# Seven products of half blocks in place of eight, in half of the second feed-forward product

## The chip, the cores and the metric

The kernel runs on one core of one Trainium2 chip. The metric is the device time of one execution in microseconds. Matrix products run on TensorE (PE in the rows; its weight loads are PEld), sums and differences mostly on VectorE (DVE), activations and copies on ScalarE (ACT); GpSimd (POOL) does little here. The weights are loaded by DMAs that SyncE's queue (SP) issues.

## The reference

Two layers, each a mixer and a feed-forward part, and a last RMSNorm, on x of 256 tokens by 1024 in float32. The mixer (dilated attention and an mLSTM, gated and merged) is untouched. The part that the change is about:

```python
SEQ, D_MODEL, D_FF, DEPTH = 256, 1024, 4096, 2
h2 = rms_norm(x, norm_mlp_w)
x = x + jnp.square(jax.nn.relu(h2 @ w_ff1)) @ w_ff2
```

`w_ff1` is 1024 x 4096, `w_ff2` is 4096 x 1024, of their own in each layer.

## The kernel before

**Products in three parts.** Each float32 operand of a large product is split into hi (a copy rounded to fp32r) and lo (the rest), and a product of two tiles is three matmuls: lo of the activations with hi of the weights, hi with hi, and hi with lo of the weights.

**Steps.** All large products go through one list of steps, each one weight tile of 128 x 2 x 512 elements (512 KB). `loads` (L403) issues its DMA into one of 6 buffers `raw`, `highs` (L429) makes `hi` on ScalarE, `lows` (L436) makes `lo` on VectorE, each in one of 5 buffers (`N_SPLIT`, `N_RAW`, L24), and TensorE runs the step's matmuls. So `hi` of step i waits until TensorE has finished step i - 5, and a load waits until `lo` has been made of the tile six before. All three walk the list in its order.

**The feed-forward part.** The hidden layer is cut into 8 blocks f of 512. The first product (`by_feature`, L446) keeps the weights stationary and streams the 256 tokens: 4 steps of 24 matmuls with 256 columns for a block, into two PSUM banks. `ff_evac` (L996) takes Relu and Square on ScalarE and splits the result into hi and lo tiles of the slot X. The second product (`by_token`, L487, with `token_products`, L478) keeps the hidden tiles stationary and streams 512 columns of `w_ff2`: per block 2 column halves c by 2 steps, each step 12 matmuls of 512 columns (2 token halves t, 2 tiles of the hidden dimension, 3 parts). It accumulates over all 8 blocks into four banks. The loop at L1147 interleaves: the second product of f, then the first of f + 2. `ff2_evac` adds the four sums to x, scaled by `r2`, the norm's factor per token.

**The order.** A planner in the kernel's own Python code sets each engine's order when the kernel is built. `Scheduler` (L257) holds tasks written as generators, `Plan` (L83) and `Timed` (L158) put a time on each instruction, and the earliest ready one is issued, with ranks among those that are near. An `Any` lets the planner choose the engine of a copy. On the chip each engine runs its list in that order, and semaphores make it wait for data and buffers.

## Time and profile before

| | us |
|---|---|
| median of 3 runs | 759.64 (759.34 to 759.66) |
| the profiled execution | 759.58 |
| its span, first to last instruction | 757.8 |
| TensorE busy | 749.6 |
| VectorE busy | 491.8 |
| ScalarE busy | 417.8 |

The page gives the busy time of each engine in the span, and in 40 slices of it. A matmul's row lasts longer than the distance to the next, because matmuls overlap in the array, so what one costs is read from starts. A row of waits says which engine's instruction ended an idle time. All instructions bear one line, L199 (a helper records them), so groups are told apart by their tiles.

### The profile page before, as it was taken

The page shows a single profiled execution, that of the slowest core. Times are in us where ns is not written, and L with a number is a line of the kernel's source. Part 1 is how long each engine was busy: PE and PEld are TensorE (multiplying, and loading weights), DVE is VectorE, ACT ScalarE, POOL GpSimd, SP SyncE. Part 2 cuts the span into 40 slices and gives each one's busy share as a digit, 9 for nine tenths or more (in the row PEclk, how much of TensorE's full clock was granted, in tenths as well). Part 3 has the DMA queues.
Part 4 walks back from the last instruction along what each step waited for, and adds up shares of the span by engine and source line. Part 5 has one row for each costly group of instructions (what it writes and reads, how often), then busy time and mean ns, then how long its engine had stood idle before and what let it go on. Part 6 is the DMA issues. An engine that isn't in the chain of part 4 may idle for free.

```text
span 757.8 us, 13082 instructions
## 1 busy us (share of the span) xinstructions
PE 749.6 (99%) x5195; PEld 689.0 (91%) x5195; DVE 491.8 (65%) x750; ACT 417.8 (55%) x662; POOL 53.3 (7%) x106
## 2 busy tenths in 40 slices
PE   9999999999999999999999999999999999999996
PEld 8989889998999988899899898899989899998895
DVE  5897986568664455555568988856766655445554
ACT  6657776445554445554456467745454654445552
POOL 4764010000000000000000000000000000000000
PEclk9999999999999999999999999999999999999999
DMA  9866554555456555555654654355565555555511
GB/s 309 287 193 210 171 155 140 186 179 190 169 175 203 181 190 195 181 185 191 194 164 127 216 179 139 117 177 181 186 209 184 180 188 189 191 182 189 194 57 55
DMA packets 71260, 136.16 MB, mean 180 GB/s; under 512 B 4792, under 2 KB 6752, under 8 KB 71200
## 3 DMA queue, kind: packets, MB, share of 16 engines
q1 hardware_dynamic: 69984, 133.63, 54.3%
q0 software_dynamic: 912, 1.41, 0.8%
q8 instruction: 40, 0.66, 0.3%
q10 hardware_dynamic: 304, 0.30, 0.1%
q14 instruction: 20, 0.16, 0.1%
HBM read 133.74 MB, written 1.05 MB: 178 GB/s over the span
## 4 chain that ended last, share of the span: by engine, by line
PE 97%; ACT 1%; DVE 1%; DMA 0%; SPq 0%; issue 0%; POOLq 0%; POOL 0%; DVEq 0%
PE bank L199 97%; DMA x<-in_x 0%; DVE x L199 0%; ACT hi L199 0%; ACT big L199 0%; ACT sg L199 0%; SPq L199 0%; DVE lo L199 0%; ACT slot0h L199 0%; DVE sg L199 0%; POOL small L199 0%; POOLq L1324 0%; DVE big L199 0%; DVE small L199 0%; DVEq L1324 0%
## 5 line engine op out<-in xcount | busy, mean ns | idle before, releaser
L199 DVE TENSOR_TENSOR lo<-raw,hi 128x1024 fp32r<-128x1024 f32 (+3 forms) x251 | 304.2, 1213 | 215.0 <-ACT hi L199 214.1
L199 ACT ACTIVATE hi<-raw 128x1024 fp32r<-128x1024 f32 (+3 forms) x251 | 262.7, 1048 | 269.9 <-PE bank L199 245.1
L199 PE MATMUL bank<-slot1l,hi 128*128 128x256 f32 x576 | 162.7, 282 | 0.0
L199 PE MATMUL bank<-slot1h,hi 128*128 128x256 f32 x576 | 162.4, 282 | 0.0
L199 PE MATMUL bank<-slot1h,lo 128*128 128x256 f32 x576 | 162.3, 282 | 0.0
L199 PE MATMUL bank<-slot0h,hi 128*128 128x256 f32 x576 | 161.7, 283 | 0.2 <-ACT hi L199 0.2
L199 PE MATMUL bank<-slot0h,lo 128*128 128x256 f32 x576 | 161.0, 283 | 0.2 <-DVE lo L199 0.2
L199 PE MATMUL bank<-slot0l,hi 128*128 128x256 f32 x576 | 161.0, 282 | 0.0
L199 PEld LDWEIGHTS bank<-slot1h,hi 128*128 128x128 f32 x576 | 108.4, 188 | 1.0 <-issue 0.5
L199 PEld LDWEIGHTS bank<-slot0h,hi 128*128 128x128 f32 x576 | 107.9, 188 | 1.4 <-ACT hi L199 0.4
L199 PEld LDWEIGHTS bank<-slot1l,hi 128*128 128x128 f32 x576 | 108.3, 188 | 0.8 <-issue 0.3
L199 PEld LDWEIGHTS bank<-slot1h,lo 128*128 128x128 f32 x576 | 108.5, 188 | 0.2 <-issue 0.2
L199 PEld LDWEIGHTS bank<-slot0h,lo 128*128 128x128 f32 x576 | 107.6, 188 | 0.9 <-issue 0.5
L199 PEld LDWEIGHTS bank<-slot0l,hi 128*128 128x128 f32 x576 | 107.9, 188 | 0.5 <-issue 0.2
L199 PE MATMUL bank<-hi,slot1h 128*128 128x512 f32 (+2 forms) x228 | 85.9, 377 | 0.0
L199 PE MATMUL bank<-hi,slot1l 128*128 128x512 f32 (+2 forms) x228 | 85.5, 375 | 0.0
L199 PE MATMUL bank<-lo,slot1h 128*128 128x512 f32 (+2 forms) x228 | 85.5, 375 | 0.0
L199 PE MATMUL bank<-hi,slot0h 128*128 128x512 f32 (+1 forms) x224 | 85.2, 380 | 0.0
L199 PE MATMUL bank<-lo,slot0h 128*128 128x512 f32 (+1 forms) x224 | 84.9, 379 | 0.0
L199 PE MATMUL bank<-hi,slot0l 128*128 128x512 f32 (+1 forms) x224 | 84.8, 379 | 0.0
L199 PEld LDWEIGHTS bank<-lo,slot1h 128*128 128x128 f32 x228 | 42.8, 188 | 8.2
L199 PEld LDWEIGHTS bank<-hi,slot1h 128*128 128x128 f32 x228 | 42.8, 188 | 8.1 <-issue 0.3
(156 smaller groups left out, 718.7 us busy)
## 6 DMA issues: line engine op xcount, KB each, us to landing
raw<-in_w_ff SPq DMA_DIRECT2D x128, 512.0 KB
raw<-in_w_in SPq DMA_DIRECT2D x78, 512.0 KB
raw<-in_w_out SPq DMA_DIRECT2D x16, 512.0 KB
raw<-in_w_in SPq DMA_DIRECT2D x8, 520.0 KB
raw<-in_w_proj_mlstm SPq DMA_DIRECT2D x8, 512.0 KB
raw<-in_w_proj_att SPq DMA_DIRECT2D x8, 512.0 KB
raw<-in_w_in SPq DMA_DIRECT2D x3, 256.0 KB
x<-in_x SPq DMA_DIRECT2D x3, 256.0 KB
```

Of the source, the lines that this page charges most:

```text
L199: f(*args, **kw)
```

## The change

The 512 hidden units of a block, the 256 tokens and the 1024 output columns are each halved. Then the second product of a block is a 2 x 2 matrix of half blocks (128 tokens by 256 hidden units) times a 2 x 2 matrix of half blocks (256 by 512): eight half-block products of 6 matmuls each. For the blocks f = 0, 2, 4, 6 (`BY_SEVEN`) the kernel now uses Winograd's form of Strassen's scheme: seven products of sums of half blocks. Odd blocks stay as they were.

- The four half blocks of the hidden layer are written by Square into `mqk` (free in this part of the layer); `sums` makes four differences and sums of them on VectorE, 256 columns each, and splits all seven stationary operands into `q_h` (in the place of `zc`) and `q_l` (in the place of `sg0`), in a piece of four and one of three. There is one `q_h` and one `q_l`: the next even block waits until the last product has been made.
- The weights of a block are four tiles b11, b12, b21, b22. Three of the seven products take them as loaded (b11, b22, b21), one takes b12 + b22 (t3, formed in b12's `raw` buffer), three take running sums in `mog` (t1 = b11 + b12, t2 = t1 + b22, t4 = t2 + b21). `weight_sums` forms these four on VectorE, 1024 columns each. Each of the seven is a step of its own with a hi and a lo, and 6 matmuls.
- The products accumulate over the even blocks into seven banks, so that one bank is left. After the last even block `flush` combines P1, P6, P7 and p5 and adds them to x: three copies on ScalarE, four sums and four updates of x on VectorE. The banks of p2, p3 and p4 go on as accumulators of the odd blocks, with one more.
- The first product of blocks 2 to 7 is done in half blocks of 256 hidden units (`by_feature_half`): 2 steps of 24 matmuls, one bank, weight tiles loaded as 128 x 4 x 256 (runs of 1 KB where there were 2 KB).
- The order of steps, for f = 0, 2, 4: half block of f + 2, b11, t1, half, t3, b22, half, t2, b21, half, t4. For f = 6 the place of the halves is taken by the second product of blocks 1 and 3; blocks 5 and 7 follow. In each layer only the planner's numbers for step lengths (`new_step`) and tiles that share a place (`Tenants`) are new besides. In the last layer the final norm's weights are loaded after `flush`.

The core of the diff:

```diff
+    def by_feature_half(w, c0, xs, st, evac):
+        xh, xl = xs
+        for q in range(2):
+            def fn(i, hi, lo, q=q):
+                if q == 0:
+                    st["b"], = yield Take(banks)
+                yield Need(("hi", i))
+                order = [(kt, blk, n) for blk in range(2) for kt in range(4) for n in range(3)]
+                for j, (kt, blk, n) in enumerate(order):
+                    at["part"] = j / len(order)
+                    if n == 2:
+                        yield Need(("lo", i))
+                    k = 4 * q + kt
+                    yield mm(st["b"][:, blk * S:(blk + 1) * S], (hi, hi, lo)[n][:, kt, blk * P:(blk + 1) * P],
+                             (xh, xl, xh)[n][:, k, :], q == 0 and blk == 0 and kt == 0 and n == 0,
+                             q == 1 and kt == 3 and n == 2)
+                if q == 1:
+                    add(evac(st["b"]), 1)
+            src = w.rearrange("(k p) c -> p k c", p=P)[:, 4 * q:4 * q + 4, c0:c0 + 256]
+            new_step(src, lambda t: flat_of(t)[:, 0:1024].rearrange("p (k c) -> p k c", k=4), 2.84, fn)
...
-        hid = lambda f: tuple(s[:, 4 * (f % 2):4 * (f % 2) + 4, :] for s in X)
+        def hidden():
+            yield Need(*[tag(f"mix{k}") for k in range(4)])
+            shared.hidden()
+            mark(tag("hidden"))
+        def hid(f):
+            if f in shared.hid:
+                return shared.hid[f]
+            return tuple(s[:, 4 * (f // 2 - 2):4 * (f // 2 - 2) + 4, :] for s in X)
...
+        q_all = mqk.rearrange("p (n j) (t u) -> p (n j t) u", j=1, u=P).rearrange("p (n j) u -> p n j u", j=2)
...
-                yield act.activation(a[:], a[:], AF.Square)
-                hh, hl = (s[:, 2 * b:2 * b + 2, :] for s in hid(f))
-                yield Any(vec.tensor_copy(hh, halves(a)), act.activation(hh, halves(a), AF.Copy))
-                yield vec.tensor_tensor(hl, halves(a), hh, op=OP.subtract)
+                if f in BY_SEVEN:
+                    if f > BY_SEVEN[0]:
+                        yield Need(tag(f"q{f - 2}"))
+                    part = a.rearrange("p (j t u) -> p t j u", j=2, t=2)
+                    yield act.activation(q_all[:, 0:8:7] if b == 0 else q_all[:, 1:3], part, AF.Square)
+                else:
+                    yield act.activation(a[:], a[:], AF.Square)
+                    yield Need(tag("hidden"))
+                    hh, hl = (s[:, 2 * b:2 * b + 2, :] for s in hid(f))
+                    yield Any(vec.tensor_copy(hh, halves(a)), act.activation(hh, halves(a), AF.Copy))
+                    yield vec.tensor_tensor(hl, halves(a), hh, op=OP.subtract)
...
+        def sums(f):
+            yield Need(tag("hidden"), tag(f"f{f}0"), tag(f"f{f}1"), *([tag(f"seven{f - 2}")] if f > BY_SEVEN[0] else []))
+            q = [q_all[:, n] for n in range(8)]
+            yield vec.tensor_tensor(q[3], q[7], q[2], op=OP.subtract)
+            yield vec.tensor_tensor(q[6], q[0], q[7], op=OP.subtract)
+            yield vec.tensor_tensor(q[4], q[3], q[0], op=OP.subtract)
+            yield vec.tensor_tensor(q[5], q[4], q[1], op=OP.add)
+            for a, b in ((0, 4), (4, 7)):
+                yield Any(act.activation(shared.q_h[:, a:b], q_all[:, a:b], AF.Copy), vec.tensor_copy(shared.q_h[:, a:b], q_all[:, a:b]))
+                yield vec.tensor_tensor(shared.q_l[:, a:b], q_all[:, a:b], shared.q_h[:, a:b], op=OP.subtract)
+            mark(tag(f"q{f}"))
+        def weight_sums(f, i, raw):
+            b11, b12, b21, b22 = (wide(512)(raw[n].raw) for n in ("b11", "t3", "b21", "b22"))
+            total = wide(512)(mog)
+            yield Need(("raw", i["b11"]), ("raw", i["b12"]), *([("lo", seven[f - 2]["t4"])] if f > BY_SEVEN[0] else []))
+            yield vec.tensor_tensor(total, b11, b12, op=OP.add)
+            mark(("raw", i["t1"]))
+            yield Need(("raw", i["b22"]))
+            yield vec.tensor_tensor(b12, b12, b22, op=OP.add)
+            mark(("raw", i["t3"]))
+            yield Need(("lo", i["t1"]))
+            yield vec.tensor_tensor(total, total, b22, op=OP.add)
+            mark(("raw", i["t2"]))
+            yield Need(("lo", i["t2"]), ("raw", i["b21"]))
+            yield vec.tensor_tensor(total, total, b21, op=OP.add)
+            mark(("raw", i["t4"]), tag(f"t4{f}"))
+        def by_seven(f):
+            i = {}
+            seven[f] = i
+            last = f == BY_SEVEN[-1]
+            def one(name, product, n, src=None, raw=None):
+                def fn(k, hi, lo):
+                    yield Need(tag(f"q{f}"))
+                    if product not in prods:
+                        prods[product], = yield Take(banks)
+                    o, new = prods[product], f == BY_SEVEN[0]
+                    yield Need(("hi", k))
+                    order = [(j, part) for j in range(2) for part in range(2)] + [(j, 2) for j in range(2)]
+                    for at_, (j, part) in enumerate(order):
+                        at["part"] = at_ / 6
+                        if part == 2:
+                            yield Need(("lo", k))
+                        yield mm(o[:], (shared.q_l, shared.q_h, shared.q_h)[part][:, n, j, :], (hi, hi, lo)[part][:, j, :],
+                                 new and at_ == 0, last and at_ == 5 and product not in ("p2", "p3", "p4"))
+                    if name == "t4":
+                        mark(tag(f"seven{f}"))
+                        if last:
+                            add(flush(), 1.5)
+                step = new_step(src, wide(512), 1.395, fn, raw)
+                i[name] = step.i
+                return step
+            def w(kp, c):
+                return rows(w_ff2[l], 4 * f + 2 * kp, 512 * c, 512)
+            todo = (("b11", "P1", 0, w(0, 0), None), ("t1", "p5", 3, None, mog), ("t3", "P7", 6, w(0, 1), None),
+                    ("b22", "p3", 5, w(1, 1), None), ("t2", "P6", 4, None, mog), ("b21", "p2", 1, w(1, 0), None),
+                    ("t4", "p4", 2, None, mog))
+            at_begin, made = len(steps) - 6, {}
...
+            for k, what in enumerate(todo):
+                made[what[0]] = one(*what)
+                if k in (1, 3, 5, 6):
+                    if k == 6:
+                        made["b11"].free = [("lo", i["b11"]), ("raw", i["t1"])]
+                        made["b22"].free = [("lo", i["b22"]), ("raw", i["t3"]), ("raw", i["t2"])]
...
+        def flush():
+            yield Need(tag("hr"))
+            s1, s5, s7 = yield Take(bigs, 3)
+            for s_, name in ((s1, "P1"), (s5, "p5"), (s7, "P7")):
+                yield act.activation(s_[:], prods[name][:], AF.Copy)
+            y, = yield Take(bigs)
+            def more(t, c, v):
+                xs = x[:, t, c * 512:(c + 1) * 512]
+                return vec.scalar_tensor_tensor(xs, v, r2[:, t:t + 1], xs, op0=OP.mult, op1=OP.add)
+            yield vec.tensor_tensor(y[:], prods["P6"][:], s1[:], op=OP.add)
+            yield more(0, 0, s1[:])
+            yield vec.tensor_tensor(s1[:], s5[:], y[:], op=OP.subtract)
+            yield more(0, 1, s1[:])
+            yield vec.tensor_tensor(y[:], y[:], s7[:], op=OP.add)
+            yield more(1, 0, y[:])
+            yield vec.tensor_tensor(s5[:], s5[:], y[:], op=OP.subtract)
+            yield more(1, 1, s5[:])
+            bigs.give(s1, s5, s7, y)
+            banks.give(*(prods[name] for name in ("P1", "P6", "P7", "p5")))
+            mark(tag("flush"))
         def ff2_evac(c):
             def evac(t, w_i, bk):
                 xs = x[:, t, c * 512:(c + 1) * 512]
-                yield Need(tag("hr"))
+                yield Need(tag("flush"))
                 yield vec.scalar_tensor_tensor(xs, bk[:], r2[:, t:t + 1], xs, op0=OP.mult, op1=OP.add)
...
-        for f in range(8):
-            fl = lambda kp, f=f: [tag(f"f{f}{kp}")]
-            if l + 1 == DEPTH and f == 7:
-                by_token_last(w_ff2[l], hid(f), [out_norm(c) for c in range(2)], acc, 4 * f, fl)
-                continue
...
+        def ff_half(f, b):
+            by_feature_half(w_ff1[l], 512 * f + 256 * b, Y, {}, lambda bk: ff_evac(f)(b, bk))
...
+        def whole(f, c):
+            fl = lambda kp: [tag(f"f{f}{kp}")]
+            if f == 1:
+                starts.append((len(steps), given(c)))
+            by_token(w_ff2[l], 512 * c, 512, lambda: hid(f), (0, 1), ff2_evac(c), acc[c], begin=f == 1, end=f == 7, k0=4 * f,
+                     flags=fl)
...
+        for f in BY_SEVEN:
+            starts.append((len(steps), lambda f=f: add(sums(f), 0.4)))
+        seven_of = {f: by_seven(f) for f in BY_SEVEN}
+        for f in BY_SEVEN[:3]:
+            ff_half(f + 2, 0)
+            for g, b in ((f + 2, 1), (f + 3, 0), (f + 3, 1)):
+                next(seven_of[f])
+                ff_half(g, b)
+            next(seven_of[f])
+        whole(1, 0)
+        next(seven_of[6])
+        whole(1, 1)
+        next(seven_of[6])
+        whole(3, 0)
+        next(seven_of[6])
+        whole(3, 1)
+        next(seven_of[6])
+        for c in range(2):
+            whole(5, c)
+        if l + 1 < DEPTH:
             for c in range(2):
-                by_token(w_ff2[l], 512 * c, 512, hid(f), (0, 1), ff2_evac(c), acc[c], begin=f == 0, end=f == 7,
-                         k0=4 * f, flags=fl)
-            if f + 2 < 8:
-                by_feature(w_ff1[l], 512 * (f + 2), Y, (0, 1, 2, 3), 0, 3, {}, ff_evac(f + 2))
+                whole(7, c)
+        else:
+            by_token_last(w_ff2[l], lambda: hid(7), [out_norm(c) for c in range(2)], acc, 28, lambda kp: [tag(f"f7{kp}")])
```

How this moves instructions. On TensorE, where the second product of f = 0 begins in layer 0: `slot0h`, `slot0l` are the hidden tiles, `hi` and `lo` the weights; `slot1` is the first product's input. Before:

```order
L199 MATMUL bank5_71<-slot1l_115,hi2_101 128x256
L199 MATMUL bank5_71<-slot1h_114,lo2_106 128x256
L199 MATMUL bank3_69<-hi3_102,slot0l_113 128x512
L199 MATMUL bank3_69<-hi3_102,slot0h_112 128x512
L199 MATMUL bank3_69<-lo3_107,slot0h_112 128x512
```

After, at the end of the first half block and in the products b11 and t1 (`sg0` is `q_l`, `zc` is `q_h`):

```order
L203 MATMUL bank4_70<-hi0_99,sg0_7_2043 128x512
L203 MATMUL bank4_70<-hi0_99,zc_6_2042 128x512
L203 MATMUL bank4_70<-lo0_104,zc_6_2042 128x512 x2
L203 MATMUL bank1_67<-hi1_100,sg0_7_2043 128x512
L203 MATMUL bank1_67<-hi1_100,zc_6_2042 128x512
```

A product of two hidden tiles by 512 columns is now 6 matmuls into one bank, the four with hi first, then the two with lo; half blocks of the first product (`slot1`) stand between pairs of products.

On VectorE, around the second product of f = 2 in layer 0. Before there are the splits of weights and hidden tiles alone:

```order
L199 TENSOR_TENSOR lo2_106<-raw3_96,hi2_101 128x2x512
L199 CAST slot0h_112<-big2_76 128x512
L199 TENSOR_TENSOR slot0l_113<-big2_76,slot0h_112 128x512
L199 TENSOR_TENSOR lo3_107<-raw4_97,hi3_102 128x2x512
L199 TENSOR_TENSOR slot0l_113<-big3_77,slot0h_112 128x512
L199 TENSOR_TENSOR lo4_108<-raw5_98,hi4_103 128x2x512
```

After (`mog<-raw,raw` is t1, `raw<-raw,raw` is t3, `mog<-mog,raw` is t2, `mqk<-mqk` the hidden sums, `sg0<-mqk,zc` the first piece of `q_l`):

```order
L203 TENSOR_TENSOR lo4_108<-raw3_96,hi4_103 128x1024
L203 TENSOR_TENSOR mog_118<-raw4_97,raw1_94 128x2x512
L203 TENSOR_TENSOR lo0_104<-raw4_97,hi0_99 128x2x512
L203 TENSOR_TENSOR raw1_94<-raw1_94,raw2_95 128x2x512
L203 TENSOR_TENSOR mqk_117<-mqk_117 128x256 x3
L203 TENSOR_TENSOR lo1_105<-mog_118,hi1_100 128x2x512
L203 TENSOR_TENSOR mqk_117<-mqk_117 128x256
L203 TENSOR_TENSOR mog_118<-mog_118,raw2_95 128x2x512
L203 TENSOR_TENSOR sg0_7_2043<-mqk_117,zc_6_2042 128x1024
L203 TENSOR_TENSOR lo2_106<-raw5_98,hi2_101 128x1024
```

Between the lo of two weight tiles there now stand weight sums, the hidden sums and the lo of the hidden sums; the lo of t1 (`lo1_105<-mog_118`) and the first piece of `q_l` come behind the sum t3.

On ScalarE, at the same handover. Before:

```order
L199 ACTIVATE hi4_103<-raw1_94 128x2x512
L199 ACTIVATE big0_74<-bank0_66 128x512
L199 ACTIVATE big0_74<-big0_74 128x512
L199 ACTIVATE big1_75<-bank6_72 128x512
L199 ACTIVATE hi0_99<-raw2_95 128x2x512
L199 ACTIVATE big1_75<-big1_75 128x512
L199 ACTIVATE slot0h_112<-big1_75 128x512
```

After (`zc<-mqk` is `q_h`, first the piece of four, then the piece of three; `hi<-mog` is the hi of t1):

```order
L203 ACTIVATE big2_76<-bank2_68 128x512
L203 ACTIVATE hi1_100<-mog_118 128x2x512
L203 ACTIVATE big2_76<-big2_76 128x512
L203 ACTIVATE hi2_101<-raw5_98 128x1024
L203 ACTIVATE zc_6_2042<-mqk_117 128x1024
L203 ACTIVATE va_9_2045<-big2_76 128x512
L203 ACTIVATE hi3_102<-raw0_93 128x1024
L203 ACTIVATE zc_6_2042<-mqk_117 128x768
```

The hi of the hidden sums stands behind Relu and Square of the last half block and the hi of two weight tiles.

## Rows read from the trace of the kernel before

**Rows 1.** The page: busy time of each engine, and TensorE's granted clock by slice.

```profile
PE 749.6 (99%) x5195; PEld 689.0 (91%) x5195; DVE 491.8 (65%) x750; ACT 417.8 (55%) x662; POOL 53.3 (7%) x106
...
PEclk9999999999999999999999999999999999999999
```

**Rows 2.** The chain in order of time: start, duration (us), what.

```profile
13.38 50.79 PE bank L199 x381
...
80.23 665.39 PE bank L199 x4574
...
745.65 0.76 DVE x L199
```

**Rows 3.** Busy time of each engine in four stretches (us, instructions in brackets).

```profile
core 0: us, PE busy (x) PEld busy (x) DVE busy (x) ACT busy (x) POOL busy (x), PEclk, DMA share, GB/s
37.00:57.00 20.00, 20.00 (x125) 17.85 (x124) 20.00 (x45) 10.89 (x15) 13.31 (x29) 1.00 0.59 184
190.00:372.00 182.00, 182.00 (x1168) 164.71 (x1167) 97.88 (x102) 93.55 (x115) 0.00 (x0) 1.00 0.57 185
229.00:274.00 45.00, 45.00 (x290) 40.70 (x289) 23.04 (x23) 22.49 (x26) 0.00 (x0) 1.00 0.61 189
562.00:745.00 183.00, 183.00 (x1172) 165.54 (x1171) 98.18 (x104) 91.86 (x114) 0.00 (x0) 1.00 0.52 166
```

**Rows 4.** TensorE in order of time: first and last of 36 successive matmuls of layer 0.

```profile
363.57 0.39 PE L199 MATMUL bank<-hi,slot0h 128*128 128x512 f32 x1
...
371.71 0.39 PE L199 MATMUL bank<-hi,slot0l 128*128 128x512 f32 x1
```

**Rows 5.** Groups by line and form: count, busy us, mean ns, idle before.

```profile
L199 DVE TENSOR_TENSOR lo<-raw,hi 128x1024 fp32r<-128x1024 f32 x238 | 291.6, 1226 | 209.7 <-ACT hi L199 208.7
L199 ACT ACTIVATE hi<-raw 128x1024 fp32r<-128x1024 f32 x238 | 251.8, 1059 | 262.4 <-PE bank L199 238.0 <-issue 13.9 <-ACT mqk L199 2.5
...
L199 ACT ACTIVATE big<-big 128x512 f32<-128x512 f32 x32 | 20.1, 628 | 0.4
L199 ACT ACTIVATE big<-bank 128x512 f32<-128x512 f32 x32 | 19.2, 599 | 9.1 <-PE bank L199 8.3
...
L199 DVE TENSOR_TENSOR slot1l<-big,slot1h 128x512 fp32r<-128x512 f32 x16 | 11.1, 692 | 0.6 <-ACT slot1h L199 0.3
...
L199 DVE SCALAR_TENSOR_TENSOR x<-bank,small,x 128x512 f32<-128x512 f32 x8 | 5.9, 748 | 5.7 <-PE bank L199 5.7
...
L199 DVE TENSOR_TENSOR zc<-zc,rot 128x1024 f32<-128x1024 f32 x4 | 4.9, 1222 | 0.0
...
L199 DVE CAST slot0h<-big 128x512 fp32r<-128x512 f32 x9 | 3.8, 426 | 3.7 <-ACT big L199 3.7
...
L199 DVE TENSOR_TENSOR e<-cst,bias 128x256 f32<-128x256 f32 x8 | 3.1, 416 | 1.4 <-POOL bias L199 1.4
```

**Rows 6.** VectorE in order of time, in the dense stretch: start, duration.

```profile
41.13 1.21 DVE L199 TENSOR_TENSOR lo<-raw,hi 128x1024 fp32r<-128x1024 f32 x1
42.26 1.67 DVE L199 SCALAR_TENSOR_TENSOR mog<-bank,small,bias 128x260 f32<-128x260 f32 x4
```

**Rows 7.** Who waited for whom, all engines and the weight queue: us, times, longest.

```profile
ACT hi L199 <- PE bank L199: 245.1, 147, 2.1
DVE lo L199 <- ACT hi L199: 214.1, 177, 2.2
...
SPq L199 <- DVE lo L199: 528.5, 216, 8.2
```

**Rows 8.** DMA: from 1 to 6 us (short runs), then the page's weight queue.

```profile
DMA packets 1379, 1.10 MB, mean 219 GB/s; under 512 B 200, under 2 KB 1149, under 8 KB 1379
...
q1 hardware_dynamic: 1082, 1.00, 65.1%
...
q1 hardware_dynamic: 69984, 133.63, 54.3%
```

**Rows 9.** DMA issues: size, and median us from issue to landing.

```profile
sg<-in_final_norm_w POOLq DMA_DIRECT2D x1, 512.0 KB, 6.1
```

## What bounds it, and what the change does to the time

> **What bounds the kernel now.** I read the page's busy shares first, then the chain of waits, then the busy time of single stretches, and last what the preparing engines wait for. TensorE is busy 749.6 of the span's 757.8 us, at full granted clock in every slice [rows 1]. The chain in order of time says the same: two long pieces of TensorE work carry it from 13.4 to 745.6 us, and what follows is an 8 us tail of VectorE, ScalarE and a store [rows 2]. In the two feed-forward stretches TensorE is busy for the whole stretch (182.00 of 182.00, 183.00 of 183.00), while VectorE is busy for about 98 us of each and ScalarE for 92 to 94 [rows 3]. So a matmul taken away there is time taken away, provided that no new wait appears; and an instruction added on VectorE is free as long as it is done before TensorE asks.
>
> How far ahead are the others? ScalarE's split into hi waits 147 times for a matmul to free a buffer, VectorE's lo waits for that hi, and the weight queue waits for lo [rows 7]. All three run as far ahead as their buffers let them. Between 37 and 57 us VectorE is busy for the full 20.00 us and TensorE still doesn't idle [rows 3]: a full VectorE alone doesn't stop this kernel. That row speaks for the change more than any other, since the change lives on VectorE's slack.
>
> **The change, term by term.** The sum is made against the profiled execution, 759.58 us (span 757.8 plus 1.8 around it), which lies 0.06 under the median of the runs.
>
> *Removed.* An even block f of the second product was 8 half-block products of 6 matmuls (48 of 512 columns); it becomes 7 of 6 (42). There are 4 such blocks in each of 2 layers, so 48 matmuls go, 5195 to 5147 on the page. What one costs is its distance to the next, not its modelled 0.39: 36 in a row start from 363.57 to 371.71 [rows 4], 8.14/35 = 0.2326 us. The gain is 48 x 0.2326 = **11.2 us**, all of it on the bounding engine.
>
> *Added on VectorE, per layer.* Twelve more lo (7 instead of 4 weight tiles per even block) at 1.226; 16 weight sums of 1024 columns, the same kind of row as zc<-zc,rot, 1.222; 16 hidden sums of 256 columns at 0.416; eight lo pieces of the hidden sums, four of 1024 at 1.226 and four of 768, which lie between the 512 row (0.692) and the 1024 row (1.226), taken at 0.96; the flush of the products, four sums at 0.692 and four updates of x at 0.748. Gone are 8 lo of hidden tiles at 0.692 [rows 5]. That is 14.7 + 19.6 + 6.7 + 8.7 + 5.7 - 5.5 = 50 us, so VectorE goes from 98 to about 148 us in a stretch of some 177: 84% where it was 54%. The copies that change engines are within 2 us. For the 768 columns alone the Trainium skill gives a price (VectorE: DVE Perf Modes, the errata section: fp32 tensor_tensor takes (N+151)/0.96 ns); it would be an estimated 0.957, and the trace agrees with it at 1024 (1.224 against 1.226).
>
> *Added on ScalarE, per layer.* Twelve more hi at 1.059, hidden hi pieces of 1.06 and about 0.85, three copies at 0.6: some 22 us on 93 [rows 3, 5], below two thirds of the stretch. It hides.
>
> *Does VectorE keep up in the densest part?* A repeating part (f = 2, 4) is on TensorE four half blocks of the first product and 42 matmuls. From the 45.00 us that two whole f took, 96 matmuls of 512 at 0.2326 leave 22.7 us for 192 of 256 columns, 0.118 each [rows 3, 4]. So the part takes 4 x 48 x 0.118 + 42 x 0.2326 = 22.7 + 9.8 = 32.4 us. VectorE has in it 15 lo, 4 weight sums, 4 hidden sums, 2 hidden lo pieces, 2 lo and a cast of the odd block: 18.4 + 4.9 + 1.7 + 2.2 + 1.4 + 0.4 = 29.0 us, 89%. In a dense stretch the next row starts before the last one's end (1.13 us after the start of one that lasts 1.21) [rows 6], which makes it some 84%. On average it fits.
>
> *The new wait: the handover of the hidden sums.* Their hi and lo exist once. The next block's may be written only when TensorE has done the last product (t4) of the block before, and its first product (b11) needs the first piece; between them lies one half block of the first product, 48 x 0.118 = 5.7 us. Put 0 at the end of t4. ScalarE has in its order Relu, hi of t1, Square, hi of the next tile, then the hidden hi. Relu may go at -1.4 (its matmuls ended one product, 6 x 0.2326, earlier), so with 0.60 + 1.06 + 0.63 + 1.06 + 1.06 [rows 5] the hidden hi is done at about 3.0. VectorE, if on time, has after hi of t1 (done at about 0.3) the lo of t1, one hidden sum, a weight sum and then the hidden lo: 1.23 + 0.42 + 1.22, to 3.2, and 1.23 to 4.4. It is asked for at 5.7: 1.3 us to spare. At f = 0 and f = 6 a cast, or another lo, stands in front (0.43 to 1.23) and leaves a few tenths.
>
> What can make VectorE late? A tile's hi may start when the step five before it has ended, since there are five buffers, and its lo follows. For b11 that step ends at -4.2, so its lo is done at -2.0 (1.06 and 1.23 later). The next in VectorE's queue is the weight sum b12+b22, and b22's load is issued only when lo of the first half-block tile frees a buffer, at -6.2 (its step five before, t2, ends at -8.5). Behind a wait there are queued the lo of t1, the hidden sums and the hidden lo, and behind these TensorE. What a load takes to land the page doesn't show for this queue. The nearest row is the 512 KB load of the final norm on POOL's queue, 6.1 us [rows 9]; at that price b22 lands at -0.1, where it is wanted at -2.0, and 1.9 late less the 1.3 to spare leaves 0.6 a block, 8 x 0.6 = 4.8 us. The other end is the packets alone, 524 KB x 49 ns over 16 engines, 1.6 us [rows 8]; up to 5.5 it costs nothing. I take a value near the low end, because that row is of the same queue: under 0.1 a block, **0.6 us** in all.
>
> *Other edits.* The first product's loads now come as 1 KB runs, 48 loads of the same size. At the start of the kernel, where most packets are under 2 KB, the weight queue needs 0.651 x 16 x 5 us for 1.00 MB, 52 ns a KB; over the whole span 0.543 x 16 x 757.8 us for 133.63 MB, 49 [rows 8]. Six per cent on loads that take 60% of the engines hides. Seven banks held by the products leave one for the half blocks: its Relu (0.60) must be done within the 1.4 us of t4, twice a layer, and within 2.8 us elsewhere; ScalarE is idle enough, and a miss costs a few tenths, inside the 0.6. The final norm's weights are loaded after the products' flush: some 9 us of VectorE's queue after the last t4, and 6.1 to land [rows 9], against 14 us of matmuls (60 of 0.2326) to their first use. A miss of 1 us delays VectorE where no matmul waits for it any more: hidden. The 8 us tail after the last matmul has the same instructions. Nothing adds a gain of its own, so the low end is the plain removal.
>
> The sum: 759.6 - 11.2 + 0.6 = **749.0 us**.
>
> **Rivals.**
> (1) *A partial stall at the handovers*: the bound above, or VectorE behind by one long row more, 0.6 to 1.1 us a block: 753 to 757. For it: 84 to 89% on an in-order engine whose buffers allow five tiles of lead, now half as long in time for the products. Against it: 20.00 of 20.00 at 37 us without an idle TensorE [rows 3].
> (2) *VectorE becomes the bound at the handover, slower than before.* If its whole list (sum of t1, lo of b11, b12+b22, three hidden sums, then the four rows above) still stood before it when t4 ends, that is 5 long rows at 1.13, four short ones at 0.42 and the hidden lo at 1.23, 8.5 us against 5.7: 2.8 late in each of 8 blocks, 22 us, 771. It turns the sign from 11.2/8 = 1.4 us a block on, which is VectorE 2.7 us behind my table. Against it: that list can start at about -4.5, when lo of the tile before it is done (its step five before ends at -7.1), and the lead is full today [rows 7].
> (3) *The products don't run at the price of the matmuls they replace.* Their stationary side is a fresh tile that was just written, their moving side is the same weights. 336 of them would have to cost 0.033 more each, 0.266 in place of 0.2326, for no change: 759.6. No row speaks for it.
> (4) *The short runs bind the loads.* At twice the time per KB, the eight short loads of a dense part would take 8 x 0.524 MB x 98 ns/KB and the four others half of that each, in all 32 us over 16 engines, as long as TensorE's part: no lead is left, about 1 us a part, 754 to 755. The Trainium skill has that rule (Perfetto Trace Analysis, DMA Optimizations: DMAs under 2 KB carry significant overhead); by it the time would be this rival's. The trace disagrees so far, 52 against 49 ns [rows 8].
>
> **How the numbers follow.** The forecast (gain whole, up to 3 us of stalls, 748.2 to 751.5) gets 0.74, rival 1 0.12, rival 2 0.06, rival 3 0.05, rival 4 0.03. A measurement of this kernel can tell about 0.2%, 1.5 us. Faster is forecast, rivals 1 and 4, 0.89; same is rival 3, 0.05; slower 0.06. The range goes from 748.0, the plain removal with 0.4 for the runs' own spread, up through most of rivals 1 and 4, to 756.0; what is left out is 2, 3 and the top of 1.
>
> **What would show it.** Right: TensorE busy about 738 us and still without idle slices; 5147 matmuls; VectorE near 590 us, ScalarE near 460; the feed-forward stretches some 5.6 us shorter each. The handover: rows of TensorE waiting for VectorE at the first product of each even block, with hidden hi and lo (zc, sg0) as what it waits for; their sum over 8 is the 0.6, or rival 1, or 2. If the hidden lo waits for a weight sum and that for a landing, the load is the cause; if no row waits, VectorE's own list is. Rival 3 shows as product matmuls farther apart than 0.233; rival 4 as hi waiting for DMA in the feed-forward. The prediction is wrong if idle TensorE in these stretches adds up to more than 3 us, or if it waits anywhere outside them.

## The result: 747.93 us, a ratio of 0.9847

The changed kernel takes 747.93 us (747.80 to 748.02), the kernel before 759.60 in the same runs. The ratio is 0.9847, its 95% interval 0.983 to 0.9864. That is 11.7 us faster where 10.6 were forecast, and 0.07 under the range's low end of 748.0. The profiled execution took 747.88 us, with a span of 746.1.

The page of the kernel after, which answers [rows 1] and the last of [rows 8] (q1 is the weight queue):

```profile
PE 738.0 (99%) x5147; PEld 679.7 (91%) x5147; DVE 572.7 (77%) x848; ACT 446.1 (60%) x698; POOL 53.8 (7%) x106
...
PEclk9999999999999999999999999999999999999999
...
q1 hardware_dynamic: 82272, 133.63, 55.2%
```

TensorE lost the 48 matmuls and 11.6 us of busy time and is still the bound. VectorE took on 81 us and ScalarE 28, and neither shows in the time. The chain in order of time says it too (start, duration, what; as [rows 2]):

```profile
13.51 50.77 PE bank L203 x381
...
64.29 669.60 PE bank L203 x4655
...
733.92 0.76 DVE x L203
```

TensorE's long pieces run from 13.51 to 733.89, 720.38 us, where they ran from 13.38 to 745.62, 732.24 us. So 11.86 us went there, 0.7 more than 48 x 0.2326 = 11.16. What waits were there (us in total, times, longest) is three rows of the start of the kernel:

```profile
PE bank L203 <- DVE ones L203: 1.0, 1, 1.0
PE bank L203 <- ACT hi L203: 0.3, 1, 0.3
PE bank L203 <- DVE lo L203: 0.2, 1, 0.2
```

They are those of the kernel before (1.0, 0.2, 0.2). None of the eight handovers has one. Two stretches of the kernel after, for [rows 3]:

```profile
core 0: us, PE busy (x) PEld busy (x) DVE busy (x) ACT busy (x) POOL busy (x), PEclk, DMA share, GB/s
190.00:366.20 176.20, 176.20 (x1144) 160.06 (x1143) 138.37 (x151) 107.61 (x133) 0.00 (x0) 1.00 0.59 191
257.62:290.05 32.43, 32.43 (x237) 30.57 (x236) 26.91 (x30) 21.24 (x28) 0.00 (x0) 1.00 0.62 195
```

The feed-forward of layer 0, 5.8 us shorter by its first and last matmul, has VectorE at 79%. The second row is one period of the dense part, from one hidden lo to the next: 32.43 us (forecast 32.4), VectorE busy for 83% (forecast 84% by its dense spacing).

The handover from f = 0 to f = 2, TensorE, ScalarE and VectorE in order of time (start, duration):

```profile
254.35 0.28 PE L203 MATMUL bank<-slot1h,hi 128*128 128x256 f32 x1
...
260.01 0.39 PE L203 MATMUL bank<-hi,sg 128*128 128x512 f32 x1
...
256.07 1.05 ACT L203 ACTIVATE zc<-mqk 128x1024 fp32r<-128x1024 f32 x1
...
252.88 1.22 DVE L203 TENSOR_TENSOR raw<-raw,raw 128x1024 f32<-128x1024 f32 x1
...
255.02 1.21 DVE L203 TENSOR_TENSOR lo<-mog,hi 128x1024 fp32r<-128x1024 f32 x1
256.15 0.41 DVE L203 TENSOR_TENSOR mqk<-mqk 128x256 f32<-128x256 f32 x1
256.49 1.21 DVE L203 TENSOR_TENSOR mog<-mog,raw 128x1024 f32<-128x1024 f32 x1
257.62 1.21 DVE L203 TENSOR_TENSOR sg<-mqk,zc 128x1024 fp32r<-128x1024 f32 x1
```

t4 ends where the half block starts, at 254.35. Counted from there, the hidden hi (zc) is done at 2.77, the hidden lo (sg) at 4.48, and the first product asks for it at 5.66: 1.18 us to spare. The forecast said 3.0, 4.4, 5.7 and 1.3, with the same rows in the same order. That the lo came out to 0.1 is partly luck: the lo of t1 starts at 0.67, not at 0.3, and the four rows overlap by 0.07 to 0.08 us each time, which the forecast left out here. The other handovers have 1.0 (f = 0), 1.2 (f = 2 and 4) and 0.7 to 0.8 (f = 6).

Two questions were left. Is the handover really the place that decides, and by how much is it clear? And where do the 0.7 us come from?

### The profile page after: what moved, and what is told of

It is laid out like the page before. It is cut to its first block, busy times and chain, and to the rows that moved or that the text cites. A ratio compares the mean times of both kernels' runs of the same rounds, so it can differ in the third digit from the quotient of the medians.

```text
span 746.1 us, 13163 instructions
## 1 busy us (share of the span) xinstructions
PE 738.0 (99%) x5147; PEld 679.7 (91%) x5147; DVE 572.7 (77%) x848; ACT 446.1 (60%) x698; POOL 53.8 (7%) x106
## 3 DMA queue, kind: packets, MB, share of 16 engines
q1 hardware_dynamic: 82272, 133.63, 55.2%
## 4 chain that ended last, share of the span: by engine, by line
PE 98%; issue 1%; ACT 0%; DVE 0%; POOLq 0%; POOL 0%; DVEq 0%; ACTq 0%
PE bank L203 98%; ACT hi L203 0%; DVE lo L203 0%; ACT slot0h L203 0%; DVE x L203 0%; ACT big L203 0%; POOLq L1586 0%; POOL small L203 0%; DVEq L1586 0%; DVE sg L203 0%; DVE ones L203 0%; DVE small L203 0%; POOLq L203 0%; ACTq L203 0%
## 5 line engine op out<-in xcount | busy, mean ns | idle before, releaser
L203 PE MATMUL bank<-hi,sg 128*128 128x512 f32 x176 | 64.2, 394 | 0.0
L203 DVE TENSOR_TENSOR lo<-mog,hi 128x1024 fp32r<-128x1024 f32 x24 | 29.3, 1223 | 36.9 <-ACT hi L203 30.5
L203 PE MATMUL bank<-hi,slot1h 128*128 128x512 f32 (+2 forms) x132 | 48.0, 364 | 0.0
L203 PE MATMUL bank<-lo,slot1h 128*128 128x512 f32 (+2 forms) x132 | 47.7, 361 | 0.0
L203 PE MATMUL bank<-hi,slot1l 128*128 128x512 f32 (+2 forms) x132 | 47.6, 361 | 0.0
L203 PE MATMUL bank<-hi,slot0h 128*128 128x512 f32 (+1 forms) x128 | 47.3, 369 | 0.0
L203 PE MATMUL bank<-lo,slot0h 128*128 128x512 f32 (+1 forms) x128 | 47.1, 368 | 0.0
L203 PE MATMUL bank<-hi,slot0l 128*128 128x512 f32 (+1 forms) x128 | 47.0, 367 | 0.0
```

The source lines that it names most:

```text
L203: f(*args, **kw)
```

## The experiments

**The eighth product given back.** The product of tile b21 is done twice in each block:

```diff
+                    if name == "b21":
+                        order = order[:4] + order
+                        order += order[-2:]
```

> The changed kernel with the six matmuls of the product p2 (tile b21) done twice in each of the eight even blocks: 48 matmuls come back, 5195 in all, on operands that lie ready, and all sums, loads and handovers stay. (The output is wrong by one product.) Theory A, the price of the removed matmuls is the plain 0.2326 us and the rest of the gain (11.7 measured, 11.2 forecast) comes from the matmuls that stay, which start 0.1 to 0.5 ns closer: 747.9 + 48 x 0.232 = 759.1, so 0.5 under the kernel before. Theory B, the removed matmuls were worth more than 0.2326 each (0.243): the time of the kernel before, 759.6. Theory C, there are hidden stalls in the changed kernel that the longer TensorE time now covers: under 759.0.

Measured: 759.43 us (758.84 to 761.02) against 759.73 for the kernel before on the same chip, a ratio of 0.9996 (0.9987 to 1.0006). The times alone don't part A from B. The chain does (its first piece, and its long one):

```profile
13.45 50.78 PE bank L203 x381
...
64.24 680.78 PE bank L203 x4703
```

It ends at 745.02, so TensorE's part is 731.57 us. That is 11.19 more than in the changed kernel, or 0.2331 for each of the 48, and 0.67 less than in the kernel before. Theory A holds: the removed matmuls were worth the plain price, and the rest sits in those that stay. This table gives the mean distance from the start of one matmul to the start of the next of the same width, over all pairs in the trace that lie close (to 126 and 242 ns; some 3,380 and 1,030 to 1,090 pairs each), worked out from the records of each run:

| kernel | 256 columns, ns | 512 columns, ns |
|---|---|---|
| before | 117.41 | 232.42 |
| after | 117.29 | 232.26 |
| the eighth product given back | 117.30 | 232.24 |
| before, half blocks | 117.46 | 232.55 |
| before, half blocks, alternating | 117.44 | 232.58 |
| after, 512 B runs | 117.30 | 232.26 |
| after, few sums | 117.31 | 232.26 |
| before, hidden blocks moved | 117.41 | 232.16 |

Between before and after that is 0.12 ns x 3471 + 0.16 ns x 1047 = 0.42 + 0.17 = 0.6 us, which accounts for the 0.7 but for 0.1.

**Half blocks alone, in the kernel before.** Its first product's blocks 2 to 7 go as the changed kernel has them:

```diff
-                by_feature(w_ff1[l], 512 * (f + 2), Y, (0, 1, 2, 3), 0, 3, {}, ff_evac(f + 2))
+                for b in range(2):
+                    by_feature_half(w_ff1[l], 512 * (f + 2) + 256 * b, Y, {}, lambda bk, f=f, b=b: ff_evac(f + 2)(b, bk))
```

> The kernel before with one edit alone: blocks 2 to 7 of the first product go as half blocks of 256 columns, loaded as 1 KB runs, one bank each, in the order that the changed kernel has inside a half block; the second product keeps its eight half-block products. 5195 matmuls. Theory A, the half-block form brings the 256-column matmuls closer by some 0.16 ns (118.6 to 118.44 in the stretch): 1152 x 0.16 ns = 0.2 us, 759.4. Theory B, it carries the whole unexplained gain: 759.1. Theory C, the form is neutral and the closer spacing is the products' (their stationary side in other tiles): 759.6. If short runs bound the loads (rival 4), it would be slower than 759.6 by 1 us or more.

Measured: 760.06 us (759.61 to 761.51) against 759.73, ratio 1.0004 (0.9995 to 1.0012); distances 117.46 and 232.55. A and B fall: the form brings nothing. The short runs cost nothing that can be measured either.

**Alternating in shorter pieces, in the kernel before.** The same half blocks, with the second product's tiles of hidden chunks 0 and 1 ahead of the first half block and the others ahead of the second.

```diff
-            for c in range(2):
-                by_token(w_ff2[l], 512 * c, 512, hid(f), (0, 1), ff2_evac(c), acc[c], begin=f == 0, end=f == 7,
+            for b in range(2):
+                for c in range(2):
+                    by_token(w_ff2[l], 512 * c, 512, hid(f), (b,), ff2_evac(c), acc[c], begin=f == 0 and b == 0,
```

> The kernel before with half blocks in the first product (as in before_half) and the second product's tiles taken in another order, so that the two kinds alternate in shorter pieces: 24 matmuls of 512 columns, 48 of 256, 24, 48. 5195 matmuls. Theory A, it is the finer alternation that lets the matmuls of the changed kernel start closer (117.41 to 117.29 ns for 256 columns, 232.42 to 232.26 for 512): half a us under the kernel before, and these distances in the trace. Theory B, the alternation is not the cause: the distances of the kernel before, 117.4 and 232.4 to 232.5, and no time gained.

Measured: 761.01 us against 759.50, ratio 1.0013 (1.0004 to 1.0022); distances 117.44 and 232.58. Theory B: the alternation is not the cause. This order is a little slower, and one new wait of TensorE for a hidden lo (0.5 us) is part of that.

**VectorE's load taken away.** Three of the four weight sums of each block are left out:

```diff
-            yield vec.tensor_tensor(b12, b12, b22, op=OP.add)
-            yield vec.tensor_tensor(total, total, b22, op=OP.add)
-            yield vec.tensor_tensor(total, total, b21, op=OP.add)
```

> The changed kernel without three of the four weight sums of each even block (only b11+b12 is made, and stands in for the others): 24 VectorE rows of 1024 columns less, 27 to 29 us of VectorE, every load, hi, lo and matmul stays. (The output is wrong.) Theory A, VectorE's whole new load is hidden: 747.9, the distances of the matmuls as in the changed kernel. Theory B, VectorE's load costs something that shows in no wait (matmuls slowed while it works): under 747.5, with closer matmuls.

Measured: 747.95 us (747.94 to 748.38). VectorE's busy time fell from 572.7 to 550.5 us (24 rows less, four copies more, which the order moved to it), the time and the distances stayed. Theory A: these 22 of the 81 us that VectorE took on are hidden, and they neither slow nor speed TensorE's matmuls. The rest of the 81 this run leaves in place.

**Hidden blocks in other buffers, in the kernel before.** The split hidden blocks lie in zc, va and num in place of the slot:

```diff
+        both = self.lay("zc", [8, S], F32R)
+        self.hid = {0: (both[:, 0:4], both[:, 4:8]), 1: (self.lay("va", [4, S], F32R), self.lay("num", [4, S], F32R))}
```

> The kernel before, eight products, whole blocks and its order, with one edit: the split hidden blocks (the stationary side of the second product) lie where the changed kernel has them, in the buffers of the mixing stage (zc for even blocks, va and num for odd ones), and no longer in the slot whose other half-pair the first product reads. 5195 matmuls. Theory A, it is where these tiles lie that lets matmuls start closer in the changed kernel: 117.3 ns (256 columns) and 232.26 (512) in the trace and about 759.1, half a us under the kernel before. Theory B, the place is not the cause: 117.4 and 232.4, 759.6; then the cause of the half us stays open.

In its trace every engine runs the same instructions as in the kernel before, in the same order, so the tiles' place is what differs.

Measured: 759.48 us (759.23 to 762.54) against 759.58, ratio 0.9996 (0.9987 to 1.0005); distances 117.41 and 232.16. It is half an answer. The 512-column matmuls, which read these buffers, come closer by 0.26 ns (0.16 in the changed kernel); the 256-column ones, which don't, stay. So the place of the stationary tiles can account for the 0.2 us of the 512-column matmuls, by the trace and not by the times: the two kernels with half blocks moved this distance by 0.13 and 0.16 ns with the tiles left in the slot.

For the 0.4 us of the 256-column matmuls the same records show a likely cause that no run varies by itself: which of the five buffers `hi` and `lo` a step's weights lie in (step i takes buffer i mod 5). In the run with half blocks alone, the mean distance within a step of 24 matmuls is 119.5 to 120.1 ns in buffers 0 and 4 and 117.2 to 118.4 in the other three, and 19 of its 48 such steps lie in these two. In the changed kernel it is 15 of 48. At the first run's mean for each buffer that brings these steps from 118.55 to 118.39 ns; measured are 118.29. A stretch that the change doesn't touch points the same way, the 576 matmuls of 256 columns in the mixing stage. In layer 0 they take 77.76 to 77.78 us in every kernel here. In layer 1 they take 77.63 us in the four kernels with the old list of steps and 77.53 in the seven with the new one, where 12 more steps stand ahead, so that each step lies two buffers further on.

**A little more work at the handover.** One more VectorE row of 256 columns (0.34 us) ahead of each hidden lo:

```diff
+                for _ in range(1 if a == 0 else 0):
+                    yield vec.tensor_tensor(q[5], q[4], q[1], op=OP.add)
                 yield vec.tensor_tensor(shared.q_l[:, a:b], q_all[:, a:b], shared.q_h[:, a:b], op=OP.subtract)
```

> The changed kernel with one more VectorE row of 256 columns (a hidden sum done again, 0.34 us in a dense stretch) just ahead of the hidden lo at each of the eight handovers. The ledger at the handover says 1.0 to 1.2 us to spare (lo done 4.5 us after t4, asked for at 5.7): nothing, 747.9 within 0.2. If instead the handover were already the limit, 8 x 0.34 = 2.7 us more: 750.7.

Measured: 748.22 us (747.92 to 748.29), span 746.0 (746.1 in the changed kernel). Nothing, as the ledger says; no handover shows a wait, and the two in the middle of each layer still have 0.84 to 0.86 us to spare.

**More work than there is to spare.** The first hidden lo is written twice, a lo of a weight tile between the two:

```diff
-                yield vec.tensor_tensor(shared.q_l[:, a:b], q_all[:, a:b], shared.q_h[:, a:b], op=OP.subtract)
+                for _ in range(2 if a == 0 else 1):
+                    yield vec.tensor_tensor(shared.q_l[:, a:b], q_all[:, a:b], shared.q_h[:, a:b], op=OP.subtract)
```

> The changed kernel with the first hidden lo written twice at each of the eight handovers; in VectorE's order a lo of a weight tile stands between the two, so that the piece TensorE asks for is done 2 x 1.13 = 2.26 us later than now. By the ledger, with 1.0 to 1.2 to spare, TensorE stands still for 1.06 to 1.26 us at each: 8 x 1.16 = 9.3, 757.2, with waits of TensorE for VectorE at the first product of each even block and nowhere else. If VectorE's average load decides (it would go from 572.7 to 582 us of 746), nothing: 747.9. If a late VectorE is not caught up within a block, more than 9.3.

Measured: 760.31 us (759.15 to 761.45), 12.1 above the run with 0.34 us more on the same chip. Eight rows, some 10 us of VectorE's time, took back the whole gain. Who waited (us, times, longest), and one of the stops in order of time:

```profile
PE bank L203 <- DVE sg L203: 9.4, 8, 1.5
```

```profile
262.81 0.28 PE L203 MATMUL bank<-slot1h,lo 128*128 128x256 f32 x1
264.07 0.50 PE L203 MATMUL bank<-hi,sg 128*128 128x512 f32 x1 [0.98 <-DVE sg L203]
264.41 0.39 PE L203 MATMUL bank<-hi,zc 128*128 128x512 f32 x1
```

Eight stops of 9.4 us together, where 9.3 were worked out, each at the first product of an even block: VectorE late by more than the spare goes to TensorE one to one. The time rose by more than the stops, because the row's idle time isn't the whole of a stop. From 262.81 to 264.07 is 1.26 us, 1.14 more than the usual 0.12, while the row says 0.98; and the next distance is 0.34 in place of 0.23. So this stop costs 0.27 us above its idle time. The eight have 0.23 to 0.27, together 2.0, and 9.4 + 2.0 is 11.4. TensorE's work in this profiled execution, from the start of the long pieces to the last matmul, is 11.5 us longer than in the changed kernel's; the medians, 12.1 apart, are of runs that scatter by 2 us.

**The load of b22 landing later.** The load is issued twice into the same buffer, the second after the first has landed:

```diff
+            op = load(n)
+            if loaded[n].twice:
+                op.call = lambda once=op.call: (once(), once())
```

> The changed kernel with the load of tile b22 of each even block issued twice into the same buffer, the second after the first has landed; the order on every other engine is unchanged. A load issued on an idle queue lands some 3.2 us after its issue in the changed kernel's trace (issue at 212.95 us, the sum that waits for it starts at 216.56 in the nearest row, 3.6), so b22 would now land 6.4 to 6.7 us after its first issue, a little beyond the bound of 6.1 that the prediction used. Theory A, the handover's ledger with measured places (issue 5.4 before the end of t4, sum b12+b22 at -1.5, 0.8 to 1.2 us to spare at the hidden lo): the sum starts 2.4 to 2.8 us later, TensorE stands still 1.3 us at each of four middle blocks, 2.0 at each f = 6, 0.4 at each f = 0, and each stop costs 0.25 of restart: 12 us, 760. Theory B, the prediction's own term at 6.1 (0.6 a block): 752.7. Theory C, the load is off the path altogether: 747.9.

Measured: 771.89 us (770.90 to 774.31), 24 above the changed kernel; ratio to the kernel before 1.016 (1.014 to 1.018). The mechanism is A's; its 12 us were half of what was measured. Waits, then one block in order of time (weight queue, VectorE, TensorE):

```profile
PE bank L203 <- DVE sg L203: 16.8, 7, 2.9
```

```profile
DVE raw L203 <- DMA raw<-in_w_ff: 30.7, 8, 5.5
```

```profile
251.55 0.37 SPq L203 DMA_DIRECT2D raw<-in_w_ff  x1
...
259.64 1.23 DVE L203 TENSOR_TENSOR raw<-raw,raw 128x1024 f32<-128x1024 f32 x1 [4.11 <-DMA raw<-in_w_ff]
...
265.67 0.50 PE L203 MATMUL bank<-hi,sg 128*128 128x512 f32 x1 [2.92 <-DVE sg L203]
```

From the first issue to the sum it was 8.1 us, not 6.4 to 6.7: the packets of the second load take 3.1 us, those of the first 2.1, and from 257.5 us on 1 KB packets of the loads queued behind it run beside them. Put 8.1 into the prediction's own line (issue at -6.2, wanted at -2.0, 1.3 to spare) and it gives 1.9 + 2.0 - 1.3 = 2.6 us a block; with the measured places (-5.4, -1.5, 1.2) it is 2.7 + 1.5 - 1.2 = 3.0 for the block shown, which stops for 2.92. The seven stops are 2.0 to 2.9, and the eighth, another 0.7, is put down to ScalarE by its row. What is left of the 24 us is the restart, 2.1 in all eight by the distances around them, and something that no forecast had, the clock:

```profile
core 0: us, PE busy (x) PEld busy (x) DVE busy (x) ACT busy (x) POOL busy (x), PEclk, DMA share, GB/s
262.70:265.60 2.90, 0.05 (x1) 0.00 (x0) 2.90 (x5) 2.90 (x5) 0.00 (x0) 1.00 0.01 4
266.50:267.00 0.50, 0.50 (x2) 0.37 (x2) 0.50 (x2) 0.01 (x1) 0.00 (x0) 0.50 0.00 0
267.00:269.50 2.50, 2.50 (x7) 1.95 (x6) 2.50 (x4) 1.06 (x1) 0.00 (x0) 0.50 0.55 169
270.00:273.00 3.00, 3.00 (x27) 2.96 (x26) 2.76 (x3) 0.92 (x1) 0.00 (x0) 1.00 0.76 226
```

Soon after the stop, TensorE is granted half its clock, 1.2 GHz, for some 3 us before it is back at 2.4. That happened after three of the stops, at 8 matmuls x 0.195 us = 1.6 each. The sum is 16.8 + 0.7 + 2.1 + 4.7 = 24.3 us, and TensorE's work, counted as above, is 24.4 us longer.

**Shorter runs.** The half blocks' loads are cut by columns, 512 B runs in place of 1 KB:

```diff
-            src = w.rearrange("(k p) c -> p k c", p=P)[:, 4 * q:4 * q + 4, c0:c0 + 256]
+            src = w.rearrange("(k p) c -> p k c", p=P)[:, :, c0 + P * q:c0 + P * q + P]
```

> The changed kernel with the half-block loads of the first product cut the other way: all 8 k-tiles by 128 columns per load, so that runs are 512 B where they were 1 KB; bytes, loads, matmuls and VectorE's work stay. Theory A, a load's price goes by bytes, with a few per cent for short runs (52 against 49 ns per KB was the row for runs under 2 KB): nothing, 747.9 within 0.3, no new wait for a DMA in the feed-forward. Theory B, rival 4's mechanism one step further (time per run, not per byte, so that 512 B runs take twice the time per KB): the lead of the loads is used up in the dense parts, 1 us or more in each of six: 754 or more, with hi waiting for the loads.

Measured: 747.92 us (747.52 to 748.52). The weight queue on its page:

```profile
q1 hardware_dynamic: 106848, 133.63, 57.7%
```

24,576 more packets took 2.5 points more of the engines' time (55.2% in the changed kernel) and nothing of the kernel's. Theory A holds, and rival 4 is gone even one step further than the change goes.

## Why the prediction came out as it did, step by step

- *What bounds the kernel*: right. TensorE is busy for the whole of the feed-forward stretches, before and after, and a matmul removed is time removed.
- *Removed, 48 x 0.2326 = 11.2*: right. Given back, the 48 cost 11.19.
- *VectorE, 50 us a layer*: the rows were right, the price a little high. The forecast was 590 us of busy time, measured are 572.7, because rows in a dense stretch overlap (1.13 for 1.21, [rows 6]) and busy time counts the overlap once: row by row the new work is 95.5 us, in busy time 80.9. The dense part's 83% is the 84% that the prediction worked out from that spacing. ScalarE has 446 of the 460.
- *The handover*: right at f = 2 and 4 in its rows and to 0.1 us in the time to spare, where two misses cancelled (the late lo of t1, the overlap of the rows), and too careful at f = 0 and 6 (0.7 to 1.0 to spare, not a few tenths). The two experiments bound it from both sides: 0.34 us more is free, 2.26 us more costs 9.4 us of stops.
- *The load of b22, +0.6*: this term failed. It was put between 1.6 and 6.1 us for a landing. In the changed kernel sums wait for a load at f = 0 alone, and there this is the one of b22 (weight queue, then VectorE):

```profile
212.95 0.37 SPq L203 DMA_DIRECT2D raw<-in_w_ff  x1
...
216.56 1.22 DVE L203 TENSOR_TENSOR raw<-raw,raw 128x1024 f32<-128x1024 f32 x1 [0.45 <-DMA raw<-in_w_ff]
```

  At most 3.6 us, on the weight queue with little ahead of it. In the middle block above, the load is issued at 248.97, 5.4 us before the end of t4 and not 6.2. Its last packet ends at 252.23, 3.3 us later, and the sum starts at 252.88 (-1.5, not -2.0) with no wait. So the term is 0. That it was worth asking is what the doubled load shows: at 8.1 us it is 24 us.
- *"Nothing adds a gain of its own, so the low end is the plain removal"*: this step failed too. Matmuls that the change doesn't touch start 0.05 to 0.1% closer in the changed kernel, and over 4,500 of them that is 0.6 us. The cause is shown in part at most: the place of the tiles for the 512-column ones, and for the 256-column ones a likely cause, the steps' buffers, that no run varied alone. The two errors lie on the same side, and together they account for the 1.1 us by which the time came out lower. The low end had 0.4 us of room for the runs' spread and none for an error of the price itself, where 0.1% of TensorE's 750 us is already 0.75.
- *Rivals 1 and 2*: no handover waits. Rival 2's mechanism is real and its price was right in kind: 8 late handovers of a good us each take the gain back, as its point of 1.4 us a block says, and the doubled load made the kernel 12 us slower than before.
- *Rival 3*: the products' matmuls cost the plain price (0.2331 for those given back, a mean of 0.2323 over all pairs of 512 columns).
- *Rival 4*: 1 KB and 512 B runs take more packets and no time here. The Trainium skill (Perfetto Trace Analysis, DMA Optimizations) says that small DMAs, under 2 KB, have a significant overhead per transfer. The loads here are 512 KB each in short runs, so rival 4 read that rule further than it is stated; for runs, the traces don't bear it out where the queue's packets fill 55 to 58% of the engines' time.

## What to carry to other kernels

Where one engine is busy without a gap, count what is removed from it at its start-to-start distance, and spend the rest of the work on the point where the other engines hand over to it: lay their rows out in time from the last event, and compare the spare with the longest row that could slip in. Here the ledger's end held to 0.1 us, in part by misses that cancelled. With about 1 us to spare at each handover it suggests that a second step of this kind would first have to take work off VectorE; that was not tried. Draw the ends of a range with room for the price itself, not only for waits.

## What the runs showed of the hardware

- A stop of TensorE costs more than its idle row: 0.23 to 0.27 us more at each of eight stops of 1.0 to 1.5 us, by the distances of the matmuls around it.
- After three of the eight late handovers with the doubled load, stops of 2.0 to 2.9 us, TensorE ran at a granted clock of 0.50 for some 3 us, with 512-column matmuls 0.43 us apart (0.232 otherwise). After stops of like length at the others it didn't, and after the stops of 1.0 to 1.5 us it did not show, so what decides is not shown. The Trainium skill (TensorE: Matmul & The Clock Gate, "Wait — 56ns, not 53.3ns?") gives 426.7 ns from start to start for 512 columns at the lower level. The trace agrees, with 426 to 427.
- The distance of two 512-column matmuls changed by 0.1% when their stationary side was moved, in one trace each: 232.42 ns from the slot, 232.16 from zc, va and num. Why the 256-column ones come 0.1% closer in every kernel with the seven products is not shown: half blocks, their alternation, VectorE's load and the length of the runs were tried, and none is it. The buffer that holds a step's weights goes with differences up to 2.9 ns in the run with half blocks alone (117.2 in buffer 1, 120.1 in buffer 0), and is the likely cause.
